# Two transformer blocks in one launch: the opening of block 2 put in another order, and three projections with 512 channels moving

## The chip, the cores and the metric

One core of one Trainium2 chip. The metric is the device time of one execution in microseconds (us). All inputs are float32 and lie in HBM; the program runs once per launch and nothing is kept from an earlier one. In the text, PE is TensorE, PEld its weight loads, DVE VectorE, ACT ScalarE, POOL GpSimd and SP the engine that issues most of the transfers.

## The reference, cut to what matters

512 tokens of 1024 channels pass through two different blocks.

```python
# block 1
hx  = modulate(rmsnorm(x, norm1_g), sh1, sc1)
q, k, v, u, b, c, ga, gc = split(hx @ w_in)          # 6656 columns
o   = window_attention(rope(q), rope(k), v, k_ctx, v_ctx, sink)
y   = b * conv3(c * u)
x   = x + g1 * ((sigmoid(ga) * (o @ w_pa) + sigmoid(gc) * (y @ w_pc)) @ w_out)
hx2 = modulate(rmsnorm(x, norm2_g), sh2, sc2)
x   = x + g2 * moe(hx2)            # 16 experts, each takes its best 64 tokens
x   = rmsnorm(x, final_norm_g)
# block 2
h   = rmsnorm(x, norm_g)
u, v, za, ab, ag, zb, ga, gb = split(h @ w_in_2 + b_in)   # 8 x 1024 columns
ya  = gelu(u) * spatial(layernorm(gelu(v))) * silu(za)
yb  = silu(groupnorm(conv31(ab * sigmoid(ag)))) * silu(zb)
x   = x + (sigmoid(ga) * (ya @ w_pa) + sigmoid(gb) * (yb @ w_pb)) @ w_out_2
x   = x + sigmoid(rmsnorm(x, ple_g) @ w_ple_gate) * (p @ w_ple)
out = rmsnorm(x, final_g)
```

## The kernel before

Every engine's order is written out by hand: the program text is the order in which each engine gets its instructions, and waits come from the tiles that they read and write. A tile pool hands a new tile the place of an old one; whatever then writes it first waits until the old one's last reader is done.

**Products.** A float32 product is made of three: both operands are split into a high part (rounded by ACT, L250 for weights) and the rest (a DVE subtraction, L248), and `mm3` (L287 to L291) issues high times high, high times low and low times high. `gemm_ct` holds weights still and moves 512 tokens. `gemm_tc` holds 128 tokens still and moves the 256 channels of one weight tile, for which `W` (class `Weights`) loads 1 MB tiles of 1024 rows by 256 columns into two buffers (`wr`), splits them in quarters (`steps`) and loads two ahead. Three products use `gemm_tc` with two weight tiles side by side in one PSUM bank: `w_out` of block 1 (`gemm_x1`, called for n = 0, 1 and four token tiles t), and in block 2 `w_out_2` and `w_ple_gate` (`gemm_n`, through `take2` and `walk`). In each, all 8 blocks of 128 input channels of one token tile are done before the next token tile; small work is hooked in between (transposes and router sums in the first: `half_T`, `half_mm`; the norm and the transposes of x in the others: `norm3`, `put_x3`). `post_x1`, `post_x3` and `post_x4` take the results out of PSUM.

**Experts.** `eload` issues loads of 1 MB expert tiles on SP into whatever pools have free places (B, B2, wr, wh, wl and X): 16 tiles are ordered while `w_out` of block 1 runs, four more before the experts start. Behind that `pair_gemm` orders one tile for each one used. The loop over p does two experts at a time (side by side in the array): gate, up, transpose, down, with the gather for the next pair and `combine` for the pair before put between. At p == 5 `spread` (L895 to L904) makes rows out of columns on all 128 partitions: DVE makes a diagonal, PE multiplies it with ones, ACT copies the result, for `final_norm_g` and for its product with `norm_g_2`; at p == 7 again for the bias of v. The last down product (L1373) runs in two halves n of the tile `py`, and `put_y` reads half 0 while half 1 is computed.

**Opening of block 2** (L1273 to L1518). x after the experts is `acc`, four token tiles t in two halves. `x2_half` adds half n of the last experts' result (`combine_half`, DVE L1261) and squares it on ACT (L1291); `x2_sums` (DVE L1295) weighs the squares with `final_norm_g` squared. From both sums `x2_stats` and `power` (POOL L179) make the factors of both norms at once (`ae`). `h2_gain` multiplies x by both gains (L1460, two of the eight on POOL), `h2_row` by the factor (ACT L1465), `put_T` transposes it and splits it (PE L1427, ACT L1429, DVE L1430). The first product of block 2 is chunk 0 of v (`v_chunk`, 128 tokens still, 256 channels moving), whose steps are put between the four token tiles; the low parts of its weights are made on POOL. Then come ag and ab for j = 0 (`ct_chunk`, 512 tokens moving), from which on the 31 taps of the convolution run on DVE in the background (`run_bg`). `xf_gain` (POOL L1547) multiplies x by `final_norm_g` for the residual.

Of the kernel before, what the change touches and what calls it, by code (L numbers as in the profile page):

```python
# [62 lines left out]
def tile_two_blocks(ctx: ExitStack, tc: tile.TileContext, a, out):  # L63
# [131 lines left out]

    class Weights:

# [236 lines left out]
    specs += [(w_o1, 0), (w_o1, 256, "b2"), (w_o1, 512), (w_o1, 768, "b2")]  # L434
    wallocs = {}
    W = Weights(specs, wallocs)
# [274 lines left out]

    def mod_hooks(h, dst, add, after):


        w = []

        def step(k):
            if not w:
                w.append(nextw()[1])
            sc = sT[:, 4 * h + k, 0:1]  # L720
            if h or k or add:
                DVE.scalar_tensor_tensor(dst, w[0][:, k], sc, dst, op0=OP.mult, op1=OP.add)
            else:
                DVE.tensor_scalar(dst, w[0][:, k], sc, None, op0=OP.mult)

        hooks = {k: [lambda k=k: step(k)] for k in range(4)}
        if h:
            hooks[9] = [after]
        return hooks
# [166 lines left out]
    def spread(dst, cols_, tmp_):  # L896

        for n in range(2):
            d_ = tmp_()
            DVE.tensor_mul(d_.rearrange("p (a b) -> p a b", b=128), ident[:, None, :].to_broadcast([128, 4, 128]),  # L900
                           cols_[:, 4 * n:4 * n + 4, None].to_broadcast([128, 4, 128]))
            p_ = bank()
            PE.matmul(p_, one, d_, start=True, stop=True)
            ACT.activation(dst[:, n * 512:n * 512 + 512], p_, AF.Copy)  # L904

# [24 lines left out]
    wallocs["b2"] = lambda sh: (big2("wbh", sh, F32R), big2("wbl", sh, F32R))  # L930
# [4 lines left out]
    for j in range(4):  # L935
# [15 lines left out]
        for q, (xs, post) in enumerate(((hx, gate), (os_, proj_a), (hx, gate), (ys_, proj_c))):  # L951
# [8 lines left out]
            if j == 3 and q == 3:  # L960
                i0 = ci[0] + 1
                hooks = {14: [lambda: W.split(i0 + 1)]}
# [89 lines left out]
    def eload(tags):  # L1052

        for tag in tags.split():
            i = len(etiles)
            if i < len(elist):
# [44 lines left out]
    def gemm_x1(t, n, ws, hooks):  # L1101

        p_ = None
        st = 0
        cut = t == NT - 1 and n
        for c in range(2):
            p_ = bank() if cut or not c else p_
            for _ in gemm_tc(p_[:, c * 256:c * 256 + 256], ws[c], t, mg):
                for h in hooks.get(st, ()):
                    h()  # L1110
                st += 1
            if cut:
                post_x1(t, slice(n * 512 + 256 * c, n * 512 + 256 * c + 256), p_[:, 256 * c:256 * c + 256])
        if not cut:
            post_x1(t, half(n), p_)

    last = None
    for n in range(2):
        ws = [nextw()[1], nextw()[1]]
        for t in range(NT):  # L1120
            hooks = {}
            if last:
                lt, ln = last
                hooks = {3: [lambda: half_T(lt, ln)], 5: [lambda: half_mm(lt, ln)]}
                if n and t > 1:
                    hooks[1] = [lambda: router_aff(t - 2)]
            else:
                hooks = {0: [lambda: W.split(ci[0])], 2: [router_prep]}
            if n == 0 and t == 1:
                hooks[1] = [lambda: W.split(ci[0] + 1), pw_load,  # L1130
                            lambda: eload("B B B B wr wr B2 B2 wh wl wh wl B2 B2 B2 B")]
            if n and not t:
                hooks[7] = [pw_T]
            gemm_x1(t, n, ws, hooks)
            last = (t, n)
# [132 lines left out]
    def put_y(p, py, ns=(0, 1)):  # L1268

        yt = {}  # L1270
        for n in ns:
            yt[n] = tmp("yt")
            DVE.scalar_tensor_tensor(yt[n], py[:, n], gt_[:, p:p + 1], g2b[:, half(n)], op0=OP.mult, op1=OP.mult)  # L1273
# [7 lines left out]
    sq4 = cp.tile([128, NT, 2, 2], F32, name="sq4")  # L1281

    sqx = {}

    def x2_half(t, n, tile_):
        combine_half(7, t, n)
        x2_square(t, n, tile_)

    def x2_square(t, n, tile_):
        sqx[t] = tile_("sqx")  # L1290
        ACT.activation(sqx[t], arow(t, half(n)), AF.Square, scale=D ** -0.5, accum_out=sq4[:, t, n, 0:1])  # L1291

    def x2_sums(t, n):

        DVE.tensor_tensor_reduce(sqx[t], sqx[t], rows2[:, 0, half(n)], 1.0, sq4[:, t, 0, 1:2] if n else 0.0,  # L1295
                                 op0=OP.mult, op1=OP.add, accum_out=sq4[:, t, n, 1:2])

    for p in range(8):
# [18 lines left out]
        if p == 7:  # L1317
            rows2 = big("rows2", [2, D])
            DVE.tensor_mul(rows2[:, 0], fng, fng)
            side[1] = lambda: spread(rows2[:, 1], column("b_in_2", 8, 8), tmp)  # L1320
# [19 lines left out]
        if p == 5:  # L1340
            fng = gp.tile([128, D], F32, name="fng", tag="g1b")
            cst3 = cp.tile([128, CL["cmask"].start - nc0], F32, name="cst3", tag="cst2")
            g12 = small("g12", 8)
            spread(fng, column("final_norm_g", 0, 8), tmp)
            DVE.tensor_mul(g12, column("final_norm_g", 0, 8), column("norm_g_2", 0, 8))
            spread(cst3[:, 0:D], g12, tmp)
# [12 lines left out]
        i0 += 16  # L1359
        ybuf[p] = big("yb", [2, D], F32R)  # L1360
        for n in range(2):
            for q, (k0, nk) in enumerate(lasts[n]):
                if n and q == 2:
                    x2_half(0, 0, tmp)
                    for t in range(NT):
                        if t < NT - 1:
                            x2_half(t + 1, 0, tmp)
                        x2_sums(t, 0)
                tiles = [etiles[i0 + e][0] for e in range(2)]
                i0 += 2  # L1370
                for k in range(k0, k0 + nk):
                    for e in range(2):
                        PE.matmul(py[64 * e:64 * e + 64, n], hlhs(k, e), tiles[e][k - k0], start=(k == 0),  # L1373
                                  stop=(k == KT - 1), tile_position=(0, 64 * e))
            if n:

                ylast = hb[:, 0, half(1)]
                DVE.scalar_tensor_tensor(ylast, py[:, 1], gt_[:, p:p + 1], g2b[:, half(1)], op0=OP.mult, op1=OP.mult)
# [17 lines left out]
    w2 = a["w_in_2"][0]  # L1396
    U0, V0, ZA0, AB0, AG0, ZB0, GA0, GB0 = (i * D for i in range(8))
    specs = [(w2, V0)]
    for j in range(4):
        specs += [(w2, AG0 + 256 * j), (w2, AB0 + 256 * j)]  # L1400
    specs += [(w2, V0 + 256 * j) for j in range(1, 4)]
    for j in range(4):
        specs += [(w2, U0 + 256 * j), (w2, ZA0 + 256 * j)]
    for j in range(4):
        specs += [(w2, GA0 + 256 * j), (a["w_pa_2"][0], 256 * j)]
    specs += [(w2, GB0 + 256 * j) for j in range(4)]
    specs += [(w2, ZB0 + 256 * j) for j in range(4)]
    specs += [(a["w_pb_2"][0], 256 * j) for j in range(4)]
    for n in ("w_out_2", "w_ple_gate_2"):
        specs += [(a[n][0], 256 * j) + (("mx",) if j % 2 else ()) for j in range(4)]  # L1410
    W = Weights(specs, {"mx": lambda sh: (big3("wxh", sh, F32R), big("wxl", sh, F32R))})
    ci[0] = 0
    lead[0] = 1
    W.load(1)
    gg = cst3[:, 0:D]
    cmat = identr
    strip = gp.tile([128, 128], F32R, name="strip", tag="post")
    rsel = strip[0:64, 96:104]
    bvb = rows2[:, 1]

    def put_T(dst, t, row):

        for n in range(2):
            p_ = bank("pT", (4, 128))
            for i in range(4):
                c = n * 512 + i * 128
                PE.transpose(p_[:, i], row[:, c:c + 128], ident)  # L1427
# [44 lines left out]
    def w0_do(*js):  # L1472
        for j in js:
            w0[j]()
# [446 lines left out]
```

## Time and profile before

| | us |
|---|---|
| runs of the kernel before | 1718.19, 1718.56, 1715.05 |
| their median | 1718.19 |
| profiled execution, its own time | 1718.02 |
| its span, first to last instruction | 1716.3 |
| PE busy | 1669.9 |
| DVE busy | 933.4 |
| ACT busy | 585.8 |
| POOL busy | 65.9 |

The profile is of one execution. A row of the timeline gives the start, the length, the engine, the line and the shapes (out<-in), and in square brackets how long the engine was idle before it and who ended that. Neighbouring instructions of one form are merged (x16). Matmuls overlap, so the pace is read from start to start, not from the length. A float32 matmul that isn't split shows as two records. The span has these stages: block 1 up to 570 us, its `w_out` to 630, the choice of tokens to 653, the experts to 1127, the opening of block 2 to 1163, block 2 to the end.

### The profile page before, as it was taken

The numbers are of one execution on the slowest core, as the hardware profiler recorded it, in microseconds if no ns is written. First come the engines' busy times: TensorE is split into PE (matmuls) and PEld (weight loads), VectorE is DVE, ScalarE is ACT, GpSimd is POOL, SyncE is SP. The second block draws the span as 40 slices with busy tenths as digits, with TensorE's granted clock in tenths as the row PEclk, the third lists the DMA queues.
The fourth block names the chain that finished last, engine by engine and source line by source line (L and its number), as shares of the span: only waits on it lengthen the run. The fifth ranks groups of instructions, "written<-read, shape, count | busy, mean of one in ns | idle before, by whom it ended". The sixth has DMA issues, their size and how long they took to land.

```text
span 1716.3 us, 22506 instructions
## 1 busy us (share of the span) xinstructions
PE 1669.9 (97%) x9212; PEld 1204.1 (70%) x9212; DVE 933.4 (54%) x1697; ACT 585.8 (34%) x1117; POOL 65.9 (4%) x68
## 2 busy tenths in 40 slices
PE   8999999989999999999999999979999999999998
PEld 5987787767888984444444344348898888877898
DVE  4667776565663442212121221286889999955544
ACT  5454444455222331111011011043335443354333
POOL 2000000000000000000000000050000000000000
PEclk9999999999999999999999999999999999999999
DMA  9132322202553769999999999833323233233421
GB/s 364 56 123 74 123 74 99 74 25 75 172 181 113 304 256 345 360 399 419 419 418 420 419 420 418 315 100 99 97 76 98 74 98 99 79 118 99 144 102 50
DMA packets 168028, 334.55 MB, mean 195 GB/s; under 512 B 6927, under 2 KB 103988, under 8 KB 167668
## 3 DMA queue, kind: packets, MB, share of 16 engines
q1 hardware_dynamic: 165520, 328.50, 51.6%
q0 software_dynamic: 1024, 2.37, 0.4%
q10 hardware_dynamic: 1380, 2.23, 0.4%
q8 instruction: 72, 1.18, 0.3%
q14 instruction: 32, 0.26, 0.0%
HBM read 328.89 MB, written 4.19 MB: 194 GB/s over the span
## 4 chain that ended last, share of the span: by engine, by line
PE 90%; DVE 6%; ACT 2%; issue 1%; DMA 1%; SPq 0%; POOL 0%; POOLq 0%; DVEq 0%; ACTq 0%
PE pb L289 16%; PE pb L290 15%; PE pb L291 15%; PE pu L1238 6%; PE py L1238 6%; PE pg L1202 4%; PE po L831 2%; PE pT L823 2%; PE s L792 1%; PE pg L1259 1%; PE pv L291 1%; PE py L1373 1%; PE pa__6640 L1238 1%; PE pa__6106 L1238 1%; PE pa__5837 L1238 1%
## 5 line engine op out<-in xcount | busy, mean ns | idle before, releaser
L248 DVE TENSOR_TENSOR wl<-wr,wh 128x512 fp32r<-128x512 f32 x316 | 225.2, 731 | 95.0 <-ACT wh L250 95.0
L250 ACT ACTIVATE wh<-wr 128x512 fp32r<-128x512 f32 x320 | 183.0, 620 | 78.8 <-PE pb L290 47.1
L1593 DVE SCALAR_TENSOR_TENSOR co<-cin,cols,co 128x512 f32<-128x512 f32 x240 | 188.3, 785 | 4.1
L289 PE MATMUL pb<-h2h,wh 128*128 128x512 f32 x448 | 177.4, 396 | 0.0
L290 PE MATMUL pb<-h2l,wh 128*128 128x512 f32 x448 | 174.9, 390 | 0.0
L291 PE MATMUL pb<-h2h,wl 128*128 128x512 f32 x448 | 174.8, 390 | 0.0
L289 PE MATMUL pb<-hxh,wh 128*128 128x512 f32 x320 | 130.5, 408 | 0.0
L290 PE MATMUL pb<-hxl,wh 128*128 128x512 f32 x320 | 125.3, 391 | 0.0
L291 PE MATMUL pb<-hxh,wl 128*128 128x512 f32 x320 | 125.2, 391 | 0.0
L1238 PE MATMUL pu<-ew,xe 128*64 128x512 f32 x512 | 114.8, 596 | 0.0
L1238 PE MATMUL py<-ew,hb 128*64 128x512 f32 x440 | 101.0, 597 | 0.0
L289 PEld LDWEIGHTS pb<-h2h,wh 128*128 128x128 f32 x448 | 84.5, 189 | 19.7 <-issue 2.4
L291 PEld LDWEIGHTS pb<-h2h,wl 128*128 128x128 f32 x448 | 84.3, 188 | 17.8
L290 PEld LDWEIGHTS pb<-h2l,wh 128*128 128x128 f32 x448 | 84.3, 188 | 17.2 <-issue 0.5
L1273 DVE SCALAR_TENSOR_TENSOR yt<-py,gt__5834,g2b 128x512 f32<-128x512 f32 x15 | 10.6, 747 | 144.7 <-PE py L1238 138.3
L1238 PEld LDWEIGHTS pu<-ew,xe 128*64 128x64 f32 x512 | 35.4, 137 | 66.0 <-issue 62.9
L802 ACT ACTIVATE P<-P,m 128x512 f32<-128x512 f32 (+1 forms) x64 | 49.7, 777 | 85.8 <-DVE m L801 83.2
L798 DVE CUSTOM_DVE_ANT_0 P<-s,cst,sink 128x512 f32<-128x512 f32 (+1 forms) x64 | 52.2, 815 | 46.2 <-PE s L795 45.9
L1205 ACT ACTIVATE xe<-pg,modc,ga 128x128 f32<-128x128 f32 x64 | 25.8, 453 | 146.2 <-PE pg L1202 146.2
L1202 PEld LDWEIGHTS pg<-Gs,xr 128*128 128x128 f32 x512 | 59.5, 192 | 21.5 <-issue 19.5
L291 PEld LDWEIGHTS pb<-hxh,wl 128*128 128x128 f32 x320 | 60.2, 188 | 13.5
L289 PEld LDWEIGHTS pb<-hxh,wh 128*128 128x128 f32 x320 | 60.3, 188 | 11.4 <-issue 2.3
(468 smaller groups left out, 3305.8 us busy)
## 6 DMA issues: line engine op xcount, KB each, us to landing
ew<-w_exp_gate SPq DMA_DIRECT2D x64, 1024.0 KB, 14.2
ew<-w_exp_up SPq DMA_DIRECT2D x64, 1024.0 KB, 13.9
ew<-w_exp_down SPq DMA_DIRECT2D x59, 1024.0 KB, 14.7
wr<-w_in SPq DMA_DIRECT2D x58, 1024.0 KB, 5.6
wr<-w_mod SPq DMA_DIRECT2D x16, 1024.0 KB, 5.1
wm<-w_mod SPq DMA_DIRECT2D x8, 1024.0 KB, 11.8
wr<-w_out SPq DMA_DIRECT2D x8, 1024.0 KB, 4.9
wr<-w_proj_attn SPq DMA_DIRECT2D x4, 1024.0 KB, 5.1
```

The lines of the kernel that those rows point to most:

```text
L248: (lo_engine or DVE).tensor_tensor(lo[:, ks], raw[:, ks], hi[:, ks].bitcast(F32), op=OP.subtract)
L250: ACT.activation(hi[:, ks], raw[:, ks], AF.Copy)
L289: PE.matmul(ps, ah, bh, start=first, stop=False)
L290: PE.matmul(ps, ah, bl, start=False, stop=False)
L291: PE.matmul(ps, al, bh, start=False, stop=last)
L798: DVE.tensor_tensor_reduce(p_[:, :n], s2[:, self.s0:self.s0 + n], self.mask, 1.0, sink8[:, 4 * g + i:4 * g + i + 1], op0=OP.add, op1=OP.ma ...
L802: ACT.activation(p_[:, :n], p_[:, :n], AF.Exp, bias=m4[:, i:i + 1], scale=0.125, accum_out=sm[:, i:i + 1])
L823: PE.transpose(p_[:, i, :], self.P[i][:, kk * 128:kk * 128 + 128], ident)
L831: PE.matmul(po[64 * h:64 * h + 64], V[:, vi, g * 64:g * 64 + 64], last[:, :, h, :], start=(kk == 1), stop=(kk == nk), tile_position=(0, 64 ...
L1202: PE.matmul(p_[:, d], xrow(t, ds), Gs[p][:, t], start=(t == 0), stop=(t == NT - 1))
L1238: PE.matmul(ps[64 * e:64 * e + 64, n], lhs(k, e), tiles[e][kk][:, n * 512:n * 512 + 512], start=(k == 0), stop=(k == KT - 1), tile_positio ...
L1593: DVE.scalar_tensor_tensor(co[ct], cin[ct][:, k:k + 512], ctap(k, ct), co[ct], op0=OP.mult, op1=OP.add)
```

## The change

1. `gemm_x1`, `gemm_n`, `take2` and `walk` go. `tc512` takes their place: a weight tile is 512 rows by 512 columns (`halves`), a matmul moves 512 channels, and the token tiles of a bank are visited in an order: WIDE does the upper four blocks of input channels for all four token tiles, then the lower four; DEEP does so for token tiles 0 and 1, and then tiles 2 and 3 each on its own. With `cut` the last token tile is done in two pieces of 256 channels. The splitting of the next weights is spread over the steps.
2. Of the first 16 expert tiles 8 are ordered in the first half of `w_out`, 4 in the second half, 4 behind it; the last 14 tiles of the list don't use `wr`.
3. `spread` goes: `final_norm_g` and the bias of v come by broadcast transfers; `norm_g_2` becomes the factor of the transposed copy.
4. The last down product uses a tile of its own for half 1; the last pair's first halves are combined two by two; `strip` and `cmat` are made, and the first weights of block 2 loaded, ahead of it.
5. The opening: DVE multiplies x by `final_norm_g` into `xrow2`, ACT squares both, the factor goes into a diagonal (`x2_diag`), and a matmul with that diagonal transposes and scales at once (`h2_T`). The first product is ag for j = 0, on 512 tokens (`first_chunk`), and chunk 0 of v follows with the others. POOL keeps only `power`.

```diff
+    WIDE = [(t, h) for h in range(2) for t in range(NT)]
+    DEEP = [(0, 0), (1, 0), (0, 1), (1, 1), (2, 0), (2, 1), (3, 0), (3, 1)]
+    def tc512(xs, post, order, hooks=None, cut=False, split=True):
...
+        for u, (t, h) in enumerate(order):
+            if h not in ws:
+                i, ws[h] = nextw()
+                nxt = W.steps(i + 1) if split or not h else []
+            pieces = 2 if cut and t == NT - 1 else 1
...
+                for kk in range(4):
+                    k = 4 * h + kk
+                    mm3(p_, xs.hi(k, ts), xs.lo(k, ts), ws[h][0][:, kk, cs], ws[h][1][:, kk, cs], k == 0,
+                        k == KT - 1)
...
+                if h:
+                    post(t, cs, p_)
...
-            if i < len(elist):
+            if i < len(elist) and not (tag == "wr" and i >= len(elist) - 14):
...
+    tc512(mg, x1_put(0), WIDE,
+          {2: [router_prep], 8: [pw_load], 9: [lambda: eload("B B B B B2 B2 B2 B2")],
+           23: [lambda: half_T(0, 0)], 25: [lambda: half_mm(0, 0)], 27: [lambda: half_T(1, 0)],
+           29: [lambda: half_mm(1, 0)], 31: [lambda: half_T(2, 0)]})
+    tc512(mg, x1_put(1), DEEP,
+          {1: [lambda: half_mm(2, 0)], 3: [lambda: half_T(3, 0)], 5: [lambda: half_mm(3, 0)], 8: [pw_T],
+           15: [lambda: half_T(0, 1)], 16: [lambda: eload("wr wr wh wl")], 18: [lambda: half_mm(0, 1)],
+           20: [lambda: half_T(1, 1)], 22: [lambda: half_mm(1, 1)], 24: [lambda: router_aff(0)],
+           27: [lambda: half_T(2, 1), lambda: router_aff(1)], 29: [lambda: half_mm(2, 1)]}, True, False)
+    eload("wh wl B2 B")
...
+        DVE.tensor_mul(xrow2(t, half(n)), arow(t, half(n)), fng[:, half(n)])
+        for i, row in enumerate((arow, xrow2)):
+            ACT.activation(tile_("sqx"), row(t, half(n)), AF.Square, scale=D ** -0.5,
+                           accum_out=sq4[:, t, n, i:i + 1])
...
-            side[1] = lambda: spread(rows2[:, 1], column("b_in_2", 8, 8), tmp)
...
-            spread(fng, column("final_norm_g", 0, 8), tmp)
-            DVE.tensor_mul(g12, column("final_norm_g", 0, 8), column("norm_g_2", 0, 8))
-            spread(cst3[:, 0:D], g12, tmp)
+            ACT.dma_start(out=fng, in_=brow("final_norm_g", 0, D))
...
+        W.load(1)
+        py = [py[:, 0], bank3("py1")[:, 0]]
...
+                if n and q == 2:
+                    for t in range(2):
+                        x2_half(t, 0, tmp)
+                if n and q == 3:
+                    for t in range(2, NT):
+                        x2_half(t, 0, tmp)
...
+    def h2_T(t, k):
+        if not t:
+            hT[k] = bank("hT", (NT, 128))
+        PE.matmul(hT[k][:, t], xrow2(t, slice(k * 128, k * 128 + 128)), dg[:, t], start=True, stop=True)
+    def h2_put(k):
+        p_ = hT.pop(k).rearrange("p a b -> p (a b)")
+        g_ = column("norm_g_2", k)
+        ACT.activation(h2.hi(k), p_, AF.Copy, scale=g_)
+        DVE.scalar_tensor_tensor(h2.lo(k), p_, g_, h2.hi(k).bitcast(F32), op0=OP.mult, op1=OP.subtract)
+    K0 = 6
+    for t in range(NT):
+        x2_half(t, 1, lambda name: jk)
+        if t:
+            x2_stats(t - 1)
+        if t > 1:
+            x2_diag(t - 2)
+    h2 = Split("h2", 512)
+    for t in range(2):
+        for k in range(K0):
+            h2_T(t, k)
+    x2_stats(NT - 1)
+    x2_diag(NT - 2)
+    for k in range(K0):
+        h2_T(NT - 2, k)
+    w0_do(2)
+    x2_diag(NT - 1)
+    for k in range(K0):
+        h2_T(NT - 1, k)
+        h2_put(k)
+        if k in (1, 3):
+            w0_do(2)
+    def first_chunk(post):
...
+        for k in range(KT):
...
+            for z, (w_, x_) in enumerate(((wh, h2.hi), (wl, h2.hi), (wh, h2.lo))):
+                for m in range(2):
+                    PE.matmul(ps[m], w_[:, k, m * 128:m * 128 + 128], x_(k), start=(k == 0 and z == 0),
+                              stop=(k == KT - 1 and z == 2))
+            if k in (1, 2):
+                for t in range(NT):
+                    h2_T(t, k + 5)
+                h2_put(k + 5)
...
-    def xf_gain():
-        for t in range(NT):
-            POOL.tensor_tensor(arow(t), arow(t), fng, op=OP.mult)
...
-    for j in range(1, 4):
+    for j in range(4):
         run_bg(v_chunk(j), 0.5)
...
+    tc512(m2, lambda *x: post_x3(0, *x), WIDE)
+    tc512(m2, lambda *x: post_x3(1, *x), DEEP,
+          {14: [lambda: norm3(0)], 18: [lambda: norm3(1)], 20: [lambda: put_x3(0)], 26: [lambda: norm3(2)],
+           28: [lambda: put_x3(1)]})
...
+    tc512(x4, post_x4a, WIDE, {3: [lambda: put_x3(2)], 7: [lambda: put_x3(3)]})
+    tc512(x4, post_x4b, DEEP, None, True, False)
```

## Rows read from the trace of the kernel before

**Rows 1.** The profile page: the chain that ended last, by engine.
```profile
PE 90%; DVE 6%; ACT 2%; issue 1%; DMA 1%; SPq 0%; POOL 0%; POOLq 0%; DVEq 0%; ACTq 0%
```

**Rows 2.** Timeline of PE: 512 wide twelve steps apart, 256 wide sixteen.
```profile
560.22 0.39 PE L291 MATMUL pb<-ysh,wl 128*128 128x512 f32 x1
...
562.94 0.39 PE L291 MATMUL pb<-ysh,wl 128*128 128x512 f32 x1
...
570.77 0.28 PE L290 MATMUL pb<-wl,mgh 128*128 128x256 f32 x1
...
572.69 0.28 PE L291 MATMUL pb<-wh,mgl 128*128 128x256 f32 x1
```

**Rows 3.** The same: a slower operand, twelve steps apart.
```profile
538.84 0.39 PE L291 MATMUL pb<-osh,wl 128*128 128x512 f32 x1
...
541.64 0.39 PE L291 MATMUL pb<-osh,wl 128*128 128x512 f32 x1
```

**Rows 4.** Timeline of PE among the experts: p = 5 with spread, p = 6 without, p = 7.
```profile
985.26 0.66 PE L1334 MATMUL pg<-cst,hb 128*128 128x128 f32 x4 [0.47 <-ACT xe L1205]
...
991.15 2.04 PE L1202 MATMUL pg<-Gs,xr 128*128 128x128 f32 x16
...
1011.17 3.60 PE L1238 MATMUL pa__7462<-ew,xe 128*64 128x512 f32 x16
...
1049.08 0.66 PE L1334 MATMUL pg<-cst,hb 128*128 128x128 f32 x4 [0.47 <-ACT xe L1205]
1049.57 2.04 PE L1202 MATMUL pg<-Gs,xr 128*128 128x128 f32 x16
...
1069.59 3.60 PE L1238 MATMUL pa__7728<-ew,xe 128*64 128x512 f32 x16
...
1092.37 1.98 PE L903 MATMUL pb<-t,one 128*128 128x512 f32 x4
1094.28 3.65 PE L1238 MATMUL pu<-ew,xe 128*64 128x512 f32 x16
```

**Rows 5.** Experts' stream: windows (last: PEclk, DMA share, GB/s); issue, us to landing, from 940.
```profile
880.00:940.00 60.00, 59.22 (x307) 26.89 (x306) 11.59 (x19) 6.65 (x14) 0.00 (x0) 1.00 1.02 419
...
1105.00:1110.00 5.00, 4.09 (x22) 1.61 (x20) 1.98 (x3) 0.60 (x1) 0.00 (x0) 1.00 0.26 97
...
ew<-w_exp_gate SPq DMA_DIRECT2D x8, 1024.0 KB, 17.8
```

**Rows 6.** Timeline of PE from the last down product to the first gate product.
```profile
1116.81 3.65 PE L1373 MATMUL py<-ew,hb 128*64 128x512 f32 x16 [0.85 <-DVE yt L1273]
...
1123.16 3.65 PE L1373 MATMUL py<-ew,hb 128*64 128x512 f32 x16
1127.67 3.70 PE L1257 MATMUL pg<-hb,GT 128*128 128x512 f32 x8 [0.85 <-DVE hb L1378]
1134.81 1.27 PE L1427 MATMUL pT<-cst,hr 128*128 128x128 f32 x8 [3.44 <-ACT hr L1465]
...
1157.65 0.58 PE L291 MATMUL pv<-wh,h2l 128*128 128x256 f32 x1 [4.03 <-DVE h2l L1430]
...
1162.51 0.63 PE L289 MATMUL pb<-h2h,wh 128*128 128x512 f32 x1
```

**Rows 7.** Timelines of DVE and POOL in the opening.
```profile
1116.00 0.75 DVE L1273 SCALAR_TENSOR_TENSOR yt<-py,gt__5834,g2b 128x512 f32<-128x512 f32 x1 [6.43 <-PE py L1373]
...
1129.98 1.27 DVE L1261 TENSOR_TENSOR acc<-pg,acc 128x512 f32<-128x512 f32 x2
...
1132.63 0.16 DVE L1454 SCALAR_TENSOR_TENSOR ae<-ae,sq 128x1 f32<-128x1 f32 x1
...
1148.04 8.95 DVE L248 TENSOR_TENSOR wl<-wr,wh 128x512 fp32r<-128x512 f32 x2
...
1146.42 9.41 POOL L1547 TENSOR_TENSOR acc<-acc,fng 128x1024 f32<-128x1024 f32 x4
```

**Rows 8.** A window at the half clock (the number after POOL's is PEclk).
```profile
1156.90:1163.74 6.84, 6.09 (x25) 5.85 (x26) 3.92 (x8) 0.90 (x2) 0.00 (x0) 0.50 0.24 56
```

## What was forecast from this, before the changed kernel had run

> **What bounds the kernel now.** The profiled execution took 1718.02 us with a span of 1716.3; the median of the three runs is 1718.19, so the two can be used as one. I read the chain of waits first: PE carries 90% of it [rows 1]. So two things are worth something: fewer or shorter PE instructions anywhere, and less waiting of PE in the few stretches where the chain goes over to DVE, ACT or POOL. The timeline of PE tells which these are. It is packed among the experts but for `spread` [rows 4], and from 1163.74 us [rows 8] to its last matmul. Its one broken stretch of any size is the opening of block 2, with waits of 0.85, 0.85, 3.44 and 4.03 us among others [rows 6]. There I read DVE, POOL and the granted clock beside it [rows 7, 8].
>
> The longest wait, 4.03 us, is put down to DVE's low parts of h2 [rows 6], but DVE is late for a reason of its own: two subtractions of 0.6 us each take 8.95 us together, over the time in which POOL multiplies x by `final_norm_g`, 9.41 us [rows 7]. Behind the wait PE ran at 0.50 of its clock, 1.2 instead of 2.4 GHz, for 6.84 us [rows 8].
>
> **The parts and their prices**
>
> **1. 512 channels moving.** The three projections now issue 6 calls of `tc512`, each 4 token tiles by 8 blocks by 3 matmuls = 96 of 512 channels, where there were 192 of 256. The last token tile in the two calls with `cut` stays at 256, so 6 x 96 - 2 x 24 = 528 wide matmuls replace 1056. Wide: twelve steps take 562.94 - 560.22 = 2.72 us, 0.2267 each. Narrow: sixteen take 572.69 - 570.77 = 1.92, 0.120 each [rows 2]. A pair costs 0.240, so each wide one saves 0.0133 us, and 528 save 7.0. PE isn't waiting in these stages, so all of it counts. The lower bound is the slow wide row: (541.64 - 538.84) / 12 = 0.2333 [rows 3], which leaves 0.0067 x 528 = 3.5 us. I take 7.0, since h, x and y as operands all give 0.2267 and only one set of tiles the other.
>
> What rides on these matmuls (router sums, transposes, norms) is the same count and moves by a few matmuls, still under PE. The order WIDE needs the last blocks of the merged input about 11 us later (48 x 0.2267) than before, which can only remove a wait; half of `half_T(2, 1)`'s cover goes (12 matmuls of 0.120 instead of 24), perhaps 0.3 us. I take nothing for either. The tail behind the last matmul stays as it is: the same post work on the same 256 channels.
>
> The Trainium skill, TensorE: Matmul & The Clock Gate, section Back-to-back issue gap, gives N/2.4 + 2.5 ns from one matmul to the next: 109 ns at 256 columns and 216 at 512, by which a pair saves 2.5 ns and the change here, as an estimate, 1.3 us. The rows [rows 2] show a fixed part of about 13 ns in each matmul, not 2.5; by the page the end would come 5.7 us later than my sum.
>
> **2. `spread`.** At p = 5 the gather follows the transposes by 991.15 - 985.26 = 5.89 us, at p = 6, without `spread`, by 0.49 [rows 4]: 5.4 us. At p = 7 it takes 1094.28 - 1092.37 = 1.9. Together 7.3, on PE's path. The broadcast transfers that take its place are 0.5 MB each, on ACT's queue at p = 5 and on POOL's behind the opening; nobody waits for them soon, and behind them on their engines stands only work with microseconds to spare. So 0.
>
> Does the path get shorter, or does the stream of weights hold it? The DMA share stands at 1.02 with 419 GB/s [rows 5]: 25.2 MB for a pair of experts take 60.1 us, and PE needs 1069.59 - 1011.17 = 58.4 for one without `spread` [rows 4]. So the stream loses 1.7 us a pair. But a tile lands 17.8 us after its issue [rows 5], while it is used 20 tiles later, 20/24 of 58.4 = 48.7 us. Some 30 us are to spare, and at the end the transfers stop about 1106 [rows 5] while the last tiles are used from 1123.16 [rows 6]: 17 us. Part 2 and the 2.2 us of part 1 that fall in block 1's `w_out` use 9.5 of these, the two withheld `wr` places a tile or two of 2.5 us. It holds, narrowly at the very end, so I take the full 7.3.
>
> The 12 expert tiles ordered later than before (20 less 8) need 12 x 2.5 = 30 us of stream; 23 lie between the end of `w_out` and the experts' start, and their first product needs only the 8 that are ordered early. So 0.
>
> **3. The opening.** I count from T = 1116.00, the end of half 0 of the last down product [rows 7]. *Before*, the gate product starts at 1162.51 [rows 6] and runs at half clock to 1163.74, which costs 0.6. In front of it lies chunk 0 of v, 96 x 0.120 = 11.5 us, which the change moves behind it at full price. So without it the opening cost 1163.1 - 1116.0 - 11.5 = 35.6 us.
>
> *After*: no wait for `yt` (0.85); half 1 in two stretches of 3.65 and 3.65 and four half-0 combines in 1123.16 - 1116.81 - 3.65 = 2.7 [rows 6]: 10.0. DVE meanwhile adds and multiplies four times each at 0.6 [rows 7], about 5.5 us from 4.3 on, ending 9.8, so that the 0.75 of `ylast` ends at 10.8. Four float32 combines take 3.7 [rows 6]: 14.5. The first diagonal stands behind three adds, three multiplications (0.62 each) and seven small instructions of 0.16 [rows 7] from 11.8 on: 16.7; PE waits 2.2. `h2_T` is 32 float32 matmuls, each two records as in the gather (16 records 2.04 us, 0.12 each [rows 4]): 18 of them up to token tile 2, with the next diagonals just in time, end at 21.4, and six more at 22.9. The first copy (ACT, DVE) is done by then, and ACT and DVE need 0.6 to 0.75 a block after that, against PE's 6 x 0.2267 = 1.4. So the first chunk takes its 48 x 0.2267 = 10.9 plus eight `h2_T` at 0.24 = 1.9: it ends at 35.7. Less the chunk itself, 24.8, where it was 35.6: 10.8 gained, if the clock holds. If it falls behind the 2.2 us wait, as it did behind the 3.44 us one, a spell of 6.84 us at half costs up to 3.4 [rows 8]. I take half of that, 1.7: **9.1** us. The transposes themselves are no gain: 8 by 1.27 us before [rows 6], 8 by 1.9 now.
>
> What makes DVE's chain shorter is that POOL has only `power` left. If DVE were held up once more as in L248, by 8.95 - 1.2 = 7.7 us [rows 7], and the half clock came in full, the gain would be nil; a second such hold would make a loss of it, and nothing but the absence of long POOL work excludes that.
>
> What the move leaves late: `xf_gain`'s result is ready earlier than it was; the background taps start one chunk earlier in the order and have 16 steps more to run under; SP's load of the first weights no longer waits for the last expert tiles. No new wait that I can find stands in front of PE's later work.
>
> **Sum.** 7.0 + 7.3 + 9.1 = 23.4 us off 1718.0: **1694.6** us.
>
> **The rivals**
>
> *A. The opening gains nothing*, through DVE or the clock as bounded above. For: PE starts its first product only when all four token tiles are there, which before began with one. Against: the 9.4 us of POOL work is gone. 1718.0 - 14.3 = 1704.
>
> *B. The stream holds the experts*, and part 2's gain turns into a wait for tiles. For: DMA share 1.02. Against: the 30 us to spare. 1718.0 - 16.1 = 1702.
>
> *C. The wide matmuls save less*, 3.5 by [rows 3] instead of 7.0: 1698. The fixed part of the page named above would make this 1700; the rows speak against it.
>
> *D. Slower: the stream comes too late.* Place: the last tiles of p = 7. If the 12 late tiles and 2 withheld places all add to a stream that can't catch up (14 x 2.5 = 35 us), its end moves from 1106 to 1141, where PE, 9.5 us earlier, wants it at 1113.6: a wait of 27.4, more than the 23.4 gained: 1722. It decides from 31 us of delay on; each tile more is 2.5 us. Against: the same 20 tiles are ordered before the experts start.
>
> *E. The parts come to next to nothing*: A, B and C together leave 1718.0 - 3.5 = 1714.5.
>
> **How the numbers follow.** The forecast with its own range (1690 to 1699: the clock 1.7 either way, part 1 down to 3.5) has 0.67; A 0.11, B 0.08, C's lower end 0.07, D 0.03, E 0.04. From 1688 (a seam or two saved beyond my count) to 1704 it holds the forecast, B, C and half of A, a little over 8 in 10. About 0.2%, 3.4 us, is what a measurement here can tell from no change. Faster by more: all but D and E, 0.93; within: 0.04; slower: 0.03.
>
> **What would show it.** Right: the gather follows the transposes at p = 5 by 0.5 us; the pace in the three projections is 0.227; POOL has no long instruction behind 1100 us and no DVE instruction of 512 elements exceeds 0.8 in the opening; PE's one long wait there is about 2 us, and the first gate product ends some 35 to 39 us behind half 0. Wrong: PE waits among the experts with DMA as releaser; a pace of 0.233; a wait of over 4 us ahead of the first `h2_T`, or a half clock through the first chunk.

## The result, and the profile after

The changed kernel takes 1698.87 us (median of four runs, 1697.36 to 1699.04) where the kernel before takes 1718.31: a ratio of 0.9889, 95% interval 0.9872 to 0.9906. The forecast was 1694.6, the range 1688 to 1704. The profiled execution took 1697.36 us with a span of 1695.6. Cut at the same events in both traces, the spans differ like this (us):

| stage | before | after | forecast | measured |
|---|---|---|---|---|
| to the first matmul of block 1's `w_out` | 570.65 | 568.70 | 0 | -1.95 |
| to the first expert product | 85.85 | 84.83 | -2.2 | -1.02 |
| to the up product of p = 7 | 432.33 | 426.91 | -5.4 | -5.42 |
| to T, the end of half 0 of the last down product | 27.17 | 28.15 | -1.9 | +0.98 |
| opening: to the first gate product (before), behind the first gate chunk (after) | 46.51 | 36.77 | -9.1 | -9.74 |
| to the first matmul of `w_out_2` | 449.98 | 450.12 | 0 | +0.14 |
| to the last matmul | 96.27 | 92.64 | -4.8 | -3.63 |
| the rest | 7.54 | 7.48 | 0 | -0.06 |
| span | 1716.30 | 1695.60 | -23.4 | -20.70 |

(The opening before holds chunk 0 of v, the opening after the first gate chunk; each holds the other in the next stage.) Two rows are off by more than 1.2 us: the first, in which nothing was changed, and the fourth.

The page of the changed kernel, busy time and chain:

```profile
PE 1657.6 (98%) x8704; PEld 1173.6 (69%) x8704; DVE 917.1 (54%) x1687; ACT 582.1 (34%) x1118; POOL 49.5 (3%) x59
...
PE 90%; DVE 6%; ACT 2%; issue 1%; DMA 1%; POOL 0%; SPq 0%; POOLq 0%; ACTq 0%; DVEq 0%
```

PE's share of the chain is what it was [rows 1]; the chain as a whole is shorter. Its timeline at the wide matmuls, and at p = 5:

```profile
576.53 0.39 PE L296 MATMUL pb<-wh,mgl 128*128 128x512 f32 x1
...
579.33 0.39 PE L296 MATMUL pb<-wh,mgl 128*128 128x512 f32 x1
...
583.46 0.39 PE L296 MATMUL pb<-wh,mgl 128*128 128x512 f32 x1
...
586.18 0.39 PE L296 MATMUL pb<-wh,mgl 128*128 128x512 f32 x1
...
982.29 0.66 PE L1353 MATMUL pg<-cst,hb 128*128 128x128 f32 x4 [0.46 <-ACT xe L1211]
982.78 2.05 PE L1208 MATMUL pg<-Gs,xr 128*128 128x128 f32 x16
...
1596.62 0.39 PE L296 MATMUL pb<-wh,m2l 128*128 128x512 f32 x1
...
1599.34 0.39 PE L296 MATMUL pb<-wh,m2l 128*128 128x512 f32 x1
```

Each pair of wide rows is twelve steps (matmuls) apart. `w_out_2` runs at 2.72 / 12 = 0.2267, as the fast row of before [rows 2]. Block 1's `w_out` runs at 0.2333 first and at 0.2267 later; over the stage the mean is 0.231. At p = 5 the gather follows the transposes by 0.49 us, where it took 5.89 [rows 4].

PE at the end of p = 7, the same timeline:

```profile
1088.39 4.19 PE L1244 MATMUL pu<-ew,xe 128*64 128x512 f32 x16
...
1093.10 4.61 PE L1244 MATMUL pu<-ew,xe 128*64 128x512 f32 x16
...
1104.91 7.35 PE L1400 MATMUL py<-ew,hb 128*64 128x512 f32 x30 [0.51 <-DMA ew<-w_exp_down]
```

Sixteen such products take 3.65 elsewhere [rows 4]; here 4.19 and 4.61, and in the down product a wait has the DMA as releaser. PE runs out of tiles. The window that stands in [rows 5] for the kernel before, in the changed kernel:

```profile
880.00:940.00 60.00, 59.23 (x302) 25.90 (x300) 11.59 (x19) 6.66 (x15) 0.00 (x0) 1.00 1.03 409
```

The DMA share is full as before, but 409 GB/s come where it was 419. That was not in the forecast.

The opening, PE:

```profile
1119.41 1.13 PE L1263 MATMUL pg<-hb,GT 128*128 128x512 f32 x2 [1.17 <-DVE hb L1405]
...
1125.81 6.96 PE L1472 MATMUL hT<-dg,xf 128*128 128x128 f32 x48 [2.70 <-DVE dg L1456]
1132.52 0.72 PE L1514 MATMUL pb<-h2h,wh 128*128 128x512 f32 x2
...
1145.36 0.39 PE L294 MATMUL pb<-h2h,wh 128*128 128x512 f32 x1
```

DVE and POOL there:

```profile
1108.59 0.75 DVE L1279 SCALAR_TENSOR_TENSOR yt<-py,gt__5666,g2b 128x512 f32<-128x512 f32 x1 [7.41 <-PE py L1400]
...
1126.29 0.69 DVE L1296 TENSOR_TENSOR xf<-acc,fng 128x512 f32<-128x512 f32 x1
...
1140.13 3.09 DVE L253 TENSOR_TENSOR wl<-wr,wh 128x512 fp32r<-128x512 f32 x5
...
1123.73 0.70 POOL L179 TENSOR_TENSOR ae<-ae,mhalf 128x2 f32<-128x2 f32 x1 [492.98 <-DVE ae L1452]
```

Where PE waited eight times before, 12.8 us together (the four waits of 0.85 to 4.03 in [rows 6] among them), it waits 1.17 and 2.70. No DVE instruction of 512 elements takes over 0.75, and five in a row take 3.09, where two took 8.95 [rows 7]; POOL has nothing longer than 0.70 us of arithmetic. The first chunk ends 36.77 us behind T. Behind the two waits the clock fell here too. The first row below is of the kernel before and shows a spell behind the 3.44 us wait, beside the one of [rows 8]; the others are of the changed kernel:

```profile
1136.40:1143.30 6.90, 4.35 (x19) 4.06 (x20) 6.87 (x12) 3.59 (x8) 5.47 (x5) 0.51 0.00 0
...
1125.20:1128.70 3.50, 2.89 (x14) 2.92 (x15) 3.09 (x13) 2.59 (x7) 1.80 (x3) 0.51 0.00 0
...
1120.00:1127.00 7.00, 4.30 (x13) 2.31 (x12) 6.17 (x17) 4.98 (x14) 1.40 (x2) 0.88 0.02 6
1127.00:1134.00 7.00, 7.00 (x52) 6.74 (x50) 3.58 (x13) 3.63 (x9) 3.96 (x6) 0.88 0.44 130
1134.00:1146.00 12.00, 12.00 (x62) 10.23 (x61) 8.07 (x13) 8.23 (x15) 0.00 (x0) 1.00 0.49 159
```

So the kernel before had two spells at half clock (1.2 of 2.4 GHz) in its opening, of 6.8 us each, and the changed kernel has one of 3.4 us; through the rest of the first chunk PEclk is 1.00.

Near the end PE waits twice where it did not before, behind an ACT that has just become free:

```profile
1669.62 0.39 PE L296 MATMUL pb<-wh,x4l 128*128 128x512 f32 x1
1670.85 0.50 PE L294 MATMUL pb<-wh,x4h 128*128 128x512 f32 x1 [0.85 <-ACT wh L255]
...
1671.66 0.50 PE L295 MATMUL pb<-wl,x4h 128*128 128x512 f32 x1 [0.31 <-DVE wl L253]
...
1670.19 2.18 ACT L255 ACTIVATE wh<-wr 128x512 fp32r<-128x512 f32 x4
```

From the first of these matmuls to the third PE takes 1671.66 - 1669.62 = 2.04 us for two steps of 0.227, so 1.6 us are lost there.

### The profile page after: what moved, and what is told of

Read it like the earlier page. It is cut to its first block, busy times and chain, and to the rows that moved or that the text cites. A ratio compares the mean times of both kernels' runs of the same rounds, so it can differ in the third digit from the quotient of the medians.

```text
span 1695.6 us, 21458 instructions
## 1 busy us (share of the span) xinstructions
PE 1657.6 (98%) x8704; PEld 1173.6 (69%) x8704; DVE 917.1 (54%) x1687; ACT 582.1 (34%) x1118; POOL 49.5 (3%) x59
## 3 DMA queue, kind: packets, MB, share of 16 engines
HBM read 329.94 MB, written 4.19 MB: 197 GB/s over the span
## 4 chain that ended last, share of the span: by engine, by line
PE 90%; DVE 6%; ACT 2%; issue 1%; DMA 1%; POOL 0%; SPq 0%; POOLq 0%; ACTq 0%; DVEq 0%
PE pb L294 15%; PE pb L295 15%; PE pb L296 15%; PE pu L1244 7%; PE py L1244 6%; PE pg L1208 4%; PE po L873 2%; PE pT L865 2%; PE s L834 1%; PE pg L1265 1%; PE pv L295 1%; PE pv L296 1%; PE pv L294 1%; PE pa__5938 L1244 1%; PE pa__7273 L1244 1%
## 5 line engine op out<-in xcount | busy, mean ns | idle before, releaser
L253 DVE TENSOR_TENSOR wl<-wr,wh 128x512 fp32r<-128x512 f32 x340 | 230.1, 696 | 119.6 <-ACT wh L255 119.6
L255 ACT ACTIVATE wh<-wr 128x512 fp32r<-128x512 f32 x340 | 194.6, 620 | 104.8 <-PE pb L295 58.9
L294 PE MATMUL pb<-h2h,wh 128*128 128x512 f32 x432 | 170.8, 395 | 0.0
L296 PE MATMUL pb<-h2h,wl 128*128 128x512 f32 x432 | 168.3, 390 | 0.0
L295 PE MATMUL pb<-h2l,wh 128*128 128x512 f32 x432 | 168.2, 389 | 0.0
L294 PEld LDWEIGHTS pb<-h2h,wh 128*128 128x128 f32 x432 | 81.1, 188 | 18.9 <-issue 2.4
```

The lines of the kernel that those rows point to most:

```text
L253: (lo_engine or DVE).tensor_tensor(lo[:, ks], raw[:, ks], hi[:, ks].bitcast(F32), op=OP.subtract)
L255: ACT.activation(hi[:, ks], raw[:, ks], AF.Copy)
L294: PE.matmul(ps, ah, bh, start=first, stop=False)
L295: PE.matmul(ps, ah, bl, start=False, stop=False)
L296: PE.matmul(ps, al, bh, start=False, stop=last)
```

## The experiments

Two things were open: why PE runs out of tiles in p = 7, and what each part is worth by itself. "Loss in p = 7" below is the time from the up product of p = 7 to T less 25.13 us, which is what it takes in four runs in which no instruction there is lengthened (e7, e8, e9, e11). In the changed kernel's profile it is 28.15 - 25.13 = 3.0.

**e1: the changed kernel again.**

> The changed kernel once more, nothing edited. In its first profile the expert weights came at 409 GB/s, where the kernel before had 419, and PE lost 2.9 us to tiles in p = 7. Theory S (the stream's rate in that execution did it, whatever the code): the rate may differ this time, and the loss with it: at 419 GB/s under 1 us, at 409 again 2.5 to 3.5. Rival G (the two withheld places make the last tiles late, at any rate): 2.5 to 3.5 at either rate. Time 1697 to 1699.5 by both.

1696.93 us, ratio 0.9886 (0.987 to 0.9901). The window gave 409 GB/s again, and the loss was 26.82 - 25.13 = 1.7. That is under the 2.5 to 3.5 that both theories had, so e1 doesn't decide between them: at one rate the loss varies by more than a microsecond, and the rate doesn't.

**e2: narrow again.**

```diff
-                    mm3(p_, xs.hi(k, ts), xs.lo(k, ts), ws[h][0][:, kk, cs], ws[h][1][:, kk, cs], k == 0,
-                        k == KT - 1)
+                    for c2 in range(0, cs.stop - cs.start, 256):
+                        cn = slice(cs.start + c2, cs.start + c2 + 256)
+                        mm3(p_[:, c2:c2 + 256], xs.hi(k, ts), xs.lo(k, ts), ws[h][0][:, kk, cn],
+                            ws[h][1][:, kk, cn], k == 0 and not c2,
+                            k == KT - 1 and c2 + 256 == cs.stop - cs.start)
```

> The changed kernel with its 528 wide matmuls cut into 1056 of 256 channels again, in the new order. By the pace of the rows (0.240 for a narrow pair; wide 0.2267 in the last two projections, 0.231 in block 1's) it is slower by 352 x 0.0133 = 4.7 and 176 x 0.009 = 1.6 us, less up to 1.2 for the wait of the last weights, which a slower PE would cover, and up to 1.6 that the wait for tiles in p = 7 absorbs: +3.5 to +6.3. The forecast's part 1 as it stood: +7.0. Rival (a fixed part of 2.5 ns a matmul): +1.3 or less.

1703.15 us, ratio 0.9919 (0.9906 to 0.9931): 6.2 above e1. (The trace of the changed kernel has 360 wide matmuls in the last two projections and 168 in block 1's `w_out`, where the expectation counts 352 and 176; its sum changes by less than 0.1 us.) By stages of its profile, `w_out` of block 1 takes 86.01 - 84.81 = 1.2 longer than in e1, `w_out_2` with the gate 96.48 - 92.62 = 3.9; the waits for the last weights shrink to one of 0.42. The rest of the difference lies in stages that the edit leaves alone and that vary by as much from run to run (the start, the opening, the loss in p = 7). So the wide matmuls are worth 5.1 us here, and the rival with 1.3 falls.

**e3: the two places lent to the end.**

```diff
-            if i < len(elist) and not (tag == "wr" and i >= len(elist) - 14):
+            if i < len(elist):
```

> The changed kernel with the two places lent to the expert tiles to the end (the condition that withholds them for the last 14 tiles taken out). Theory S: the loss in p = 7 stays within 1 us of what it is without the edit, time within 1 us. Rival G: the loss goes, time down by 2 to 3 us. Either way the first weights of block 2 are ordered later, behind the last use of those places; they may land up to 10 us later than 1113 us, still ahead of the first chunk at 1132.

1696.62 us, ratio 0.9883 (0.987 to 0.9897), as e1. Its profile is of the slowest of its four runs. The loss there did not go; it was 4.0, 1.0 above the changed kernel's first profile, which is as far as theory S allowed, and 2.3 above e1:

```profile
1090.62 4.20 PE L1244 MATMUL pu<-ew,xe 128*64 128x512 f32 x16
...
1095.34 4.59 PE L1244 MATMUL pu<-ew,xe 128*64 128x512 f32 x16
...
1107.14 7.33 PE L1400 MATMUL py<-ew,hb 128*64 128x512 f32 x30 [0.52 <-DMA ew<-w_exp_down]
```

Rival G falls: with the transfers at 409 GB/s, two places more to put them in did not help.

**e4: `spread` put back** (the function as in the kernel before).

```diff
+            spread(fng, column("final_norm_g", 0, 8), tmp)
+            spread(cst3[:, 0:D], column("norm_g_2", 0, 8), tmp)
-            ACT.dma_start(out=fng, in_=brow("final_norm_g", 0, D))
...
+        if p == 7:
+            side[1] = lambda: spread(cst3[:, 0:D], column("b_in_2", 8, 8), tmp)
```

> The changed kernel with the PE broadcasts put back, two at p = 5 in place of one transfer and one at p = 7 (their results replace or are overwritten as in the kernel before; norm_g_2 stands where the product stood). The PE work is 5.4 + 1.9 = 7.3 us. Theory S: PE's delay at p = 5 gives the stream time, the wait for tiles in p = 7 shrinks by what it was (2.9), so the time goes up by about 4.4 (3.5 to 5.5). Forecast's part 2 as it stood (the stream holds, all 7.3 on the path): +7.3.

1703.36 us, ratio 0.9914 (0.9901 to 0.9928): 6.4 above e1, between theory S's 3.5 to 5.5 and the forecast's 7.3, so the whole time doesn't decide between them; the loss does. From the first expert product to T it takes 461.01, e1 453.75, the changed kernel's first profile 455.06: 7.3 and 6.0 more. The loss in p = 7 is down to 27.26 - 1.9 - 25.13 = 0.2, as theory S has it. That the sum is above 4.4 all the same can be read from the trace: the two broadcasts at p = 5 cost 65.22 - 58.38 = 6.8 here, not 5.4, since PE fell to half its clock, 1.2 of 2.4 GHz, behind the wait ahead of them (PEclk 0.67 over the window; in the kernel before it held 1.00 there). 6.8 + 1.9 less a loss of 1.5 to 2.8 gives 5.9 to 7.2, which is what was measured.

```profile
984.42 5.37 PE L945 MATMUL pb<-t,one 128*128 128x512 f32 x8 [1.47 <-DVE t L942]
```

```profile
984.40:989.60 5.20, 5.18 (x8) 1.92 (x8) 1.86 (x3) 1.79 (x3) 0.00 (x0) 0.67 1.03 410
```

**e5: the kernel before, with the long multiplication off POOL.**

```diff
-            POOL.tensor_tensor(arow(t), arow(t), fng, op=OP.mult)
+            DVE.tensor_tensor(arow(t), arow(t), fng, op=OP.mult)
```

> The kernel before with one edit: x times final_norm_g (4 instructions, 9.41 us each on POOL) goes to DVE, behind the first chunk in the program. Theory P (POOL's multiplication held DVE's two subtractions, 8.95 us for 1.2): the two subtractions take 0.6 each, PE's wait for h2's low parts falls from 4.03 to under 0.5, the half clock behind it goes, and the time falls by 4.0 (the wait alone) to 7.4 us (with half of the 6.84 us at half clock). Rival (DVE is late for another reason, or the next wait takes its place): within 1 us. This also shows the stream of the kernel before in a second execution: 419 GB/s again if its rate hangs on the code, about 409 as in the five profiles of the changed kernel's kind if it hangs on the execution or the chip.

1711.76 us, ratio 0.9963 (0.9951 to 0.9976): 6.6 under the kernel before. T to the first gate product falls from 46.51 to 39.92. In the kernel before, the two subtractions that [rows 7] shows as one row of 8.95 are 8.35 and 0.68 us long, and POOL's row of 9.41 is four multiplications of 2.3 to 2.4 us, not one (nor 9.41 each, as the expectation has it). The first row is of two subtractions with an operand in PSUM (`pT`):

```profile
1146.82 1.30 DVE L1430 TENSOR_TENSOR h2l<-pT,h2h 128x512 fp32r<-128x512 f32 x2 [1.16 <-ACT h2h L1429]
1148.04 8.35 DVE L248 TENSOR_TENSOR wl<-wr,wh 128x512 fp32r<-128x512 f32 x1
...
1156.31 0.68 DVE L248 TENSOR_TENSOR wl<-wr,wh 128x512 fp32r<-128x512 f32 x1
...
1153.49 2.34 POOL L1547 TENSOR_TENSOR acc<-acc,fng 128x1024 f32<-128x1024 f32 x1
```

In e5, DVE's subtractions and the last wait of PE there of over 0.5 us:

```profile
1145.74 0.68 DVE L248 TENSOR_TENSOR wl<-wr,wh 128x512 fp32r<-128x512 f32 x1
...
1148.71 0.68 DVE L248 TENSOR_TENSOR wl<-wr,wh 128x512 fp32r<-128x512 f32 x1
```

```profile
1140.60 0.58 PE L291 MATMUL pv<-wh,h2l 128*128 128x256 f32 x1 [1.12 <-DVE h2l L1430]
```

Theory P holds: the wait of 4.03 us is gone. One edit gives two thirds of what the whole new opening gives. The Trainium skill, SBUF — State Buffer, section SBUF: two separate sides, has DVE and POOL share a pair of ports that one instruction holds to its end, for a DVE instruction with two inputs in SBUF against POOL. The trace agrees in part: the subtraction with both inputs in SBUF was held, 8.35 us for 0.68, and the two with one in PSUM, which ran beside POOL's first multiplication, were not. But it came free only behind the last of POOL's four multiplications, at 1155.83, and not at the end of the first. Beside that, the stream of this variant ran at 419 GB/s, as in the kernel before, while every profile of the changed kernel's kind up to here had 409, and e6, from the same chip as e5, has it too. So the rate hangs on the code.

**e6: the last weights split earlier.**

```diff
-    specs += halves(a["w_out_2"][0], "mx") + halves(a["w_ple_gate_2"][0])
+    specs += halves(a["w_out_2"][0], "mx") + halves(a["w_ple_gate_2"][0], "mx")
...
-    tc512(x4, post_x4a, WIDE, {3: [lambda: put_x3(2)], 7: [lambda: put_x3(3)]})
+    tc512(x4, post_x4a, WIDE, {3: [lambda: put_x3(2)], 7: [lambda: put_x3(3)],
+                               **{s_: [last_step] for s_ in range(24, 32)}})
```

(`last_step` issues one of the eight steps of the last split: the high or the low part of a quarter of its tile.)

> The changed kernel with the last quarter of the gate weights split into tiles of its own (as the last quarter of w_out_2 is) and 8 steps earlier, ahead of the epilogues of the first half. In the profile of the changed kernel PE waits 0.85 and 0.31 us there for ACT and DVE. If the place of the split in ACT's order is what makes it late: both waits go, time down by 1.0 to 1.4 us. Rival (ACT and DVE have no time left there, so the epilogues come late instead and the tail grows by as much): no change.

Both waits go, and from the first matmul of `w_out_2` to the last of the gate it takes 90.87 instead of 92.64, 1.8 less, about what the rows above lose from start to start; the tail is as long as it was. The time, 1697.37 us (ratio 0.9879, 0.9863 to 0.9894), can't be told from e1's: its profile has a spell of lower clock at 640 to 660 us (0.91) that costs 1.6. The stage says yes, the whole time leaves it open.

**e7: a lighter stream.**

```diff
+                if 88 <= i < 96:
+                    SP.dma_start(out=t_[:, 0], in_=w[0:128])
+                    etiles.append(([t_[:, 0]] * k, tag))
+                    continue
```

> The changed kernel with half the bytes of the eight tiles of w_exp_down of p = 3 (4 MB, about 10 us of the stream) left out; those products use the first half twice, so block 1's experts 6 and 7 come out different. Theory S: PE loses nothing to tiles in p = 7 (1.9 to 3.2 us in the changed kernel's profiles), time down by 2 to 3 us. Rival (the longer instructions there are not the stream's): the loss stays, time within 1 us.

The loss is gone (25.13 from the up product to T), so the long instructions are the stream's. The time, 1697.34 (ratio 0.9876, 0.9863 to 0.989), can't be told from e1's, and the 2 to 3 us that were expected are not shown by it; in its profile, of the slowest of its four runs, the same spell at 640 to 660 us takes 1.6.

**e8, e9, e10: where the expert tiles lie.** What differs between e5 and the changed kernel for a stream that loads the same tiles? The change dropped `g12`, two buffers of 32 bytes a partition, from the pool of small constants, and the pools of the expert tiles stand behind it. Whatever else stands behind it moves along, so these runs don't tell which of the moved tiles counts. e8 puts 64 bytes back, e9 takes 64 more away, e10 takes 64 from the kernel before.

```diff
 e8
+    cp.tile([128, 16], F32, name="pad")
 e9
-    rb = cp.tile([128, 16], F32, name="rb")
+    rb = sink
 e10 (kernel before)
-            g12 = small("g12", 8)
+            g12 = rb[:, 0:8]
```

> The changed kernel with one unused tile of 64 bytes a partition in the pool of small constants. The change dropped such a tile from that pool (g12, two buffers of 8 floats), and the pool stands ahead of the pools that hold the expert tiles, so every one of these tiles begins 64 bytes lower than before. Theory A (the place of the tiles in SBUF sets the stream's rate): the stream is back at 419 GB/s, PE loses under 1 us to tiles in p = 7, time down by 1.5 to 3.5 us. Rival O (the rate hangs on the order in which the places are first filled, or on something else of the change): 409 GB/s as in the seven profiles, time within 1 us.

> The changed kernel with 64 bytes a partition less in that pool (the router's bias rb lies in the place of the attention sink, which is dead by then), so the expert tiles lie 64 bytes lower still, 128 below those of the kernel before. Theory A, if what counts is a place that is a multiple of 128 bytes: 419 GB/s or more, and no loss in p = 7; time down by 1.5 to 3.5 us. If A holds but each place has a rate of its own: any rate. Rival O: 409 GB/s.

> The kernel before with g12 in the dead place of rb, so that its pool is as large as the changed kernel's and its expert tiles begin 64 bytes lower; nothing else. Theory A: the stream falls from 419 to 409 GB/s; the time stays within 1 us, or up to 2 us slower if PE runs out of tiles at the end of p = 7 here too. Rival O: 419 GB/s, time within 1 us.

The same window of the three, in this order:

```profile
880.00:940.00 60.00, 59.22 (x309) 26.80 (x307) 11.60 (x19) 6.66 (x14) 0.00 (x0) 1.00 1.02 420
```

```profile
880.00:940.00 60.00, 59.22 (x304) 26.30 (x304) 11.59 (x19) 7.38 (x16) 0.00 (x0) 1.00 1.03 416
```

```profile
880.00:940.00 60.00, 59.22 (x304) 26.15 (x301) 11.60 (x19) 6.66 (x14) 0.00 (x0) 1.00 1.03 409
```

Theory A holds in both directions: 64 bytes bring the changed kernel to 420, and the kernel before down to 409. The 416 of e9 is less than the 419 that its expectation had if a multiple of 128 bytes were what counts. In e8 and e9 the loss in p = 7 is nil; e8's products at the place where they were lengthened:

```profile
1090.84 3.65 PE L1245 MATMUL pu<-ew,xe 128*64 128x512 f32 x16
1095.01 3.65 PE L1245 MATMUL pu<-ew,xe 128*64 128x512 f32 x16
```

e8 takes 1696.15 us (0.987, 0.9855 to 0.9886), e9 1695.01 (0.9867, 0.9853 to 0.988), e10 1718.52 (0.9999, 0.999 to 1.0007). The intervals of e8 and e9 overlap that of e1, so their whole times don't show the 1.5 us or more that theory A had; the loss in p = 7 does. e10 loses nothing in p = 7 (27.17, as the kernel before): there PE reaches the up product of p = 7 at 1089.65, 9.2 us later than in the changed kernel's first profile, and the slower stream is still in time. So the 10 GB/s cost only together with what the change gained.

**e11: e6 and e8 together.**

> The changed kernel with the 64 bytes of e8 and the earlier split of e6 together. By theory A and the stage of e6 (1.8 us less from the first to the last gate matmul): 3 to 5 us under the changed kernel, about 1693 to 1696. By rival O: the 1.8 us alone, 1695 to 1697.5.

1691.28 us, ratio 0.985 (0.9836 to 0.9863): under the expected span, with an interval wholly under e1's. Its profile has 25.13 to T and 90.85 from `w_out_2` to the last matmul. This version beats both kernels, the changed one by 5.6 to 7.6 us in the medians, but part of that is luck: its profile is 5.7 us shorter than e8's, of which e6's edit gives 1.8; 2.0 lie in the start, which no edit touches, and 1.9 in two spells at half clock that e8's profile has (in the choice of tokens and in the opening) and this one hasn't.

## Why the prediction was right, and what it missed

**The sum.** 23.4 us were forecast, 20.7 came in the profiled execution, and the median lies in the range. Of these 20.7, 1.95 stand ahead of the change: PEclk over the first 60 us is 0.97 in the profile before and 1.00 in the one after, and the profiles of the changed kernel's kind reach `w_out` at anything from 568.6 to 571.0. So the change itself gave some 18.8, and the 1.95 are luck.

**Part 1**, 7.0 forecast, 1.0 + 3.6 measured, 5.1 undone by e2. The price of a pair held where the pace was 0.2267: without the two new waits (e6) the last two projections take 96.27 - 90.87 = 5.4 us less than before, where 360 x 0.0133 = 4.8 were forecast, and the waits take 1.8 of it back. The section of the Trainium skill that the prediction names (TensorE: Matmul & The Clock Gate, Back-to-back issue gap) gives the 2.5 ns for a matmul by itself and, for a stream of pairs of weight load and matmul, 131 ns at 512 columns; the 226.7 ns of these rows agree with neither. Two things were missed. Block 1's `w_out` paces 0.231 in the mean, so the slow row [rows 3] was no oddity of one set of tiles: it came with the first four input tiles of `mg`, 0.2333, and not with the last four where nothing else stands between the matmuls. And "the tail behind the last matmul stays as it is" looked behind the last matmul only: in the order WIDE the epilogues of all four token tiles come at the end of the call, and ACT's split of the last weights is queued behind them. e6 gives this back.

**Part 2**, 7.3 forecast. PE's work went as forecast, 5.4 at p = 5 and 1.9 at p = 7; the stream took 3.0 back. The step that failed is "it holds, narrowly at the very end", and it failed by its input: the rate was read from the kernel before, 419, and taken for the chip's. At 409 a pair of experts takes 25.2 MB / 0.409 = 61.5 us against PE's 58.4, so the stream loses 3.1 a pair, not 1.7. At 419 it does hold (e8: no loss, with the same order and the two places withheld). What was put at 0 had a price as well: the broadcast transfer at p = 5, 0.5 MB in the midst of this stream, takes it 1.3 us at 409 GB/s, an estimate that no run shows by itself. The margin was smaller than said, too. The gate tiles of p = 5 in the kernel before, their issue and their first use:

```profile
912.27 21.08 SPq L1068 DMA_DIRECT2D ew<-w_exp_gate  x8
...
947.36 3.60 PE L1238 MATMUL pa__7172<-ew,xe 128*64 128x512 f32 x16
```

35.1 us, not the 48.7 of "20 tiles later": five of the 20 places are not filled again behind the first pair (the line `i not in (3, 15, 16, 17, 18)`), so some 17 us were to spare, not 30. Seven pairs lose 12 us at 419 and 22 at 409, an estimate by the figures above: the margin covers the one and not the other. Rival B, the stream, is thus what happened in part, at 3.0 of its 7.3 us. The withheld places, which the forecast and rival D counted, cost nothing that e3 could show.

**Part 3**, 9.1 forecast, 9.7 measured. 35.7 us from T to the end of the first chunk at full clock were forecast; the four profiles of this opening in which the clock held have 35.55 to 35.85. The wait ahead of `h2_T` was put at 2.2 and is 2.70. The spell at half clock was priced at 1.7, half of the 3.4 that one of 6.84 us can cost, and costs about 1.1; it is half as long, 3.4 us. Six profiles have one, and take 36.72 to 37.09. That POOL's multiplication was the cause of DVE's delay, a step argued from two rows, is shown by e5: 6.6 of the 9.7, in the kernel before. Rival A is out. Why the spell comes in six of ten executions and not in the others was not tried.

**What else was moved at no price** stayed at none: the stage behind the opening differs by 0.14 us, and the tail by 0.06.

## What to carry to other kernels

Before a schedule is planned on a stream that runs at the limit of the DMA, read its rate in the new kernel again: dropping a 64-byte constant moved every tile behind it and cost more than 2% of the rate. Count the places of a ring from a transfer's issue to its use in the trace, not from the first filling. And look at what is queued behind an epilogue on ACT when an order lets all epilogues fall due together.

## What was not expected of the hardware

The rate of 1 MB transfers from HBM, at a full DMA share, hung on where the tiles lie in SBUF: 419 to 420 GB/s at the place of the kernel before (before, e5, e8, e11), 409 at 64 bytes lower (the changed kernel, e1 to e4, e6, e10), 416 at 128 bytes lower (e9). The Trainium skill, DMA: Bandwidth & Descriptors, section How a descriptor splits into AXI transactions, has a descriptor whose start is off a multiple of 256 bytes fetch, and pay for, bytes in front of it. It speaks of what is read, while here the place that is written moved. And of two places 128 bytes apart at most one is such a multiple, yet 419 and 416 came at two such places and 409 between them, so that rule alone doesn't give these rates. A rule by steps of 128 bytes would fit them nearly, but for 416 in place of 419; more places were not tried, and the cause stays open.
